# Residual sums by accumulating transfers in a hybrid decoder layer on one core

## The chip, the core and the metric

The kernel runs on one core of a Trainium2 chip. The metric is the device time of one execution in microseconds (us), the median of several runs. One execution was profiled; its views are quoted below. PE is TensorE (PEld its weight loads), DVE is VectorE, ACT is ScalarE, POOL is GpSimd, SP is SyncE, which here issues transfers only.

## The reference, cut to what matters

One decoder layer, 1024 tokens, width 1024, all in float32:

```python
a = rmsnorm(h, ln_pre_mix)                      # h = x
q, k, v, u, z = split(a @ w_in)
groups = concat([rmsnorm(dilated_attention(q, k, v)), rmsnorm(spatial_gating(u, z, ...))])
mixed = groups @ w_out
h = h + rmsnorm(mixed, ln_post_mix)             # residual sum 1
f = rmsnorm(h, ln_pre_ffn)
g, up = split(f @ w_gate_up)
y = (silu(g) * up) @ w_down
h = h + rmsnorm(y, ln_post_ffn)                 # residual sum 2
gate = sigmoid(h @ w_pe_gate + b_pe_gate)
out = h + gate * (p @ w_pe_proj)                # residual sum 3
```

The three lines with a residual sum are what the change touches.

## The kernel before

Tokens are handled in eight tiles of 128 rows (`t` = 0 to 7), each a [128, 1024] float32 tile of 512 KB. Every float32 matrix product is made of three fast passes: an operand is split into a rounded high part and a remainder (`split`, L430: a cast on ScalarE, a subtraction on VectorE), and `mm3` (L518) multiplies high by high, high by low and low by high. The large products (input, gate-up and down projections) also use a Strassen-like scheme with seven products on half blocks (`winograd_b`). PE therefore works through some 5600 matmuls, and the other engines prepare its operands and empty its banks.

The stages follow each other: input projection; spatial gating; attention in four head pairs, each first over the first 512 tokens (`first_half`) and then over the rest (`second_half`); gate-up; down projection; and the last stage with `ffn_out` and `embed`. Into the attention other work is fed as filler: the gating half of the output projection (`gated`), the embedding projection (`ple`), and, once tokens 0 to 3 are through `h_chain`, the early gate-up products (`first_products`).

Where the residual sums are made:

- `h_chain(t)` (L1018), after `attn_out(t)` has put the mixed rows of a tile into `part[t]`. It loads x from HBM, normalises the rows (`sumsq` on ScalarE, `rstd_from` with a power on POOL, `norm_apply` on VectorE), adds x on VectorE or POOL (`EITHER`), stores h to the HBM scratch `h1d`, and normalises again for the feed-forward part. Tiles 0 to 3 come in hooks in `second_half` of head pair 0 (`TODO`), tiles 4 to 7 after the attention. `F.first` and `F.second` then transpose the result on PE.
- `ffn_out(t)` (L1261) loads h back from `h1d`, normalises the down projection's rows `y`, adds h on VectorE, transposes y on PE (8 transposes) and splits it for the gate product.
- `embed(t, nh, ...)` (L1273) makes the gate product of a tile for one half of the columns (24 matmuls of 512 columns), adds the bias, takes the sigmoid, multiplies by the embedding rows, adds h2 (`y` after its sum) on VectorE, and stores the result.

The last stage runs `ffn_out` for tiles 0 to 3, `embed` for these tiles, `ffn_out` for tiles 4 to 7, `embed` for these; the final half of tile 7 is cut in two pieces of 256 columns.

The order of instructions on each engine isn't that of the code. The program first records all operations with their dependences (`Graph.call`). `price` (L176) gives each a cost on each engine that may run it, and `order` (L224) plays the program through with these costs: on every engine it takes the first recorded operation that is ready and whose buffers are to be had. What comes out is a fixed, in-order queue for each engine. An instruction that waits on the chip longer than the planner thought holds everything behind it on its engine. A transfer on SP is priced at 0.45 us of SP, then its bytes at 330 GB/s, one after another with all other transfers, and 3.0 us until it has landed; at most 8 are kept under way.

The lines in play: `price` L176, `order` L224, `load` L416, `tt` L421, `rstd_from` L496, `sumsq` L503, `norm_apply` L508, `h_chain` L1018, `rows_out` L1180, `ffn_out` L1261, `embed` L1273. All instructions are issued from one helper line, L383 (`issue`), so that the views tell them apart by engine, tile letter and shape: m is a [128, 1024] tile, s a [128, 512] one, p a PSUM bank, t a small statistic, d an HBM scratch tensor.

Of the kernel before, what the change touches and what calls it, by code (L numbers as in the profile page):

```python
# [17 lines left out]
P = 128  # L18
S = 1024
D = 1024  # L20
NT = S // P
# [12 lines left out]
ADD, SUB, MUL = ALU.add, ALU.subtract, ALU.mult  # L34
# [79 lines left out]
class Graph:  # L114
# [61 lines left out]
    def price(self, o, outs, ins):  # L176


        o.cost, o.port, o.table, o.bytes, o.sure = {}, {}, None, 0, 0.0
        n = max([v.n for v in outs[:1] + ins[:1]])  # L180
        for e in o.engines:
            port = False
            if e == "tensor":
                n = ins[1].n
                if o.what == "transpose":
                    busy, done = 0.110, 0.27
                elif ins[0].dt == F32R:
                    busy = max(0.110, (n + 32) / 2400.0)
                    done = n / 2400.0 + 0.18
                else:  # L190
                    busy = 0.222 if n <= P else n * 4 / 2400.0
                    done = busy + 0.16
            elif e == "vector":
                tensors = [v for v in ins if v.n > 4 or n <= 4]
                busy = n / 960.0 + 0.15
                if len(ins) > len(tensors) and n > 4:
                    busy += 0.06
                if o.what == "tensor_tensor_reduce":
                    busy += 0.083
                done = busy  # L200
                busy -= 0.06
                port = n > 16 and not any(v.psum for v in tensors) and bool(tensors)
            elif e == "scalar":
                done = n / 1200.0 + (0.16 if ins[0].psum else 0.19)
                busy = done - 0.08
                if isinstance(o.kw.get("bias"), Ref):
                    done, busy = done + 0.093, busy + 0.093
                if "accum_out" in o.kw:
                    done, busy = done + 0.1, busy + 0.09
                o.table = TABLES.get(next((a for a in o.args if isinstance(a, AF)), None))  # L210
            elif e == "gpsimd":
                if n > 16:
                    busy = 2.21e-3 * n + 0.15
                else:
                    busy = 0.2 if o.what == "tensor_scalar" else 0.4 + 0.15 * n
                done, port = busy, n > 16
            else:
                size = [v for v in outs + ins if isinstance(v, Ref) and v.buf.kind in "MSTC"][0]
                o.bytes = size.n * 4 * (size.parts[1] - size.parts[0])
                busy, done = 0.45, 0.0  # L220
            o.cost[e], o.port[e] = (busy, done), port


    def order(self):  # L224
# [19 lines left out]
        port, dma, table, lanes = 0.0, 1.5, 0, [0.0] * 8  # L244
        waiting = {e: [] for e in engines}
        coming, events = [], [0.0]
        done, first, picked = [False] * n, 0, []
# [55 lines left out]
        while left:  # L303
            if not events:
                raise ValueError(f"stuck at {ops[first].what} {first}")
            now = heapq.heappop(events)
            while events and events[0] <= now + 1e-9:
                heapq.heappop(events)
            while coming and coming[0][0] <= now + 1e-9:
                _, rank, i, e = heapq.heappop(coming)  # L310
                if ops[i].start is not None:
                    continue
                bisect.insort(waiting[e], (rank, i))
            for e in engines:
                if at[e] > now + 1e-9 or not waiting[e]:
                    continue
                o = pick(e, now)
                if o is None:
                    continue
                busy, took = o.cost[e]  # L320
                o.start, o.engine = now, e
                picked.append(o)
                if o.table and o.table != table:
                    busy, took, table = busy + 1.4, took + 1.4, o.table
                at[e] = now + busy
                if e == "sync":
                    dma = max(dma, now + 0.4) + o.bytes / 330e3
                    o.end = dma + 3.0
                    lanes = lanes[1:] + [o.end]
                    at[e] = max(at[e], lanes[0])  # L330
                else:
                    o.end = now + took
                if o.port[e]:
                    port = o.end
                    heapq.heappush(events, port)
                for x in o.engines:
                    if (o.rank, o.i) in waiting[x]:
                        waiting[x].remove((o.rank, o.i))
                o.new = [b for b in o.bufs if b.slot is None]
                for b in o.new:  # L340
                    b.slot = heapq.heappop(free[b.kind])[1]
                    group[b.group] = group.get(b.group, 0) + 1
                    b.ahead = first
                    early[b.kind][first : b.born] += 1
                for b in o.bufs:
                    b.left -= 1
                    b.until = max(b.until, o.end)
                    if not b.left:
                        heapq.heappush(free[b.kind], (b.until, b.slot))
                        group[b.group] -= 1  # L350
                        live[b.kind][b.born : b.last + 1] -= 1
                        early[b.kind][b.ahead : b.born] -= 1
                        heapq.heappush(events, b.until)
                done[o.i] = True
                left -= 1
                while first < n and done[first]:
                    first += 1
                for u in o.users:
                    u.waits -= 1
                    if not u.waits:  # L360
                        release(u)
                heapq.heappush(events, at[e])
                heapq.heappush(events, now + 0.02)
# [25 lines left out]
def hybrid_block(ctx: ExitStack, tc, a, out):  # L389
    G = Graph()  # L390

    def M(dt=F32, shape=(P, 1024), group=None):
        return G.buf("M", shape, dt, group)
# [22 lines left out]
    def load(dst, src, rate=1.0):  # L416
        o = G.call("sync", "dma_start", dst, src)
        o.bytes /= rate
        return o

    def tt(dst, x, y, op=ADD, engines="vector"):  # L421
        return G.call(engines, "tensor_tensor", out=dst, in0=x, in1=y, op=op)
# [11 lines left out]
    EITHER = ("vector", "gpsimd")  # L434
# [165 lines left out]
    x = a["x"][0]  # L600
# [39 lines left out]
    ppd, h1d = DR([S, D]), DR([S, D])  # L640
# [97 lines left out]
    for q, banks in in_products(2048, 1536, zu_mm):  # L738
        for i in range(4):
            if q in (1, 6, 5):  # L740
                v, t = {1: (zs, i), 6: (us, i), 5: (us, i + 4)}[q]
# [5 lines left out]
            else:  # L747
                v = {2: zs, 3: us}.get(q, us)[i + 4 * (q == 7)]
# [4 lines left out]
            if q in (3, 4):  # L753
                t = i + 4 * (q == 4)
# [24 lines left out]
    for q, banks in in_products(0, AW, qk_mm, (1, 2, 6, 5, 3, 7, 4)):  # L779
        for i in range(4):  # L780
            dst = {1: q_part[i], 2: q_part[i], 6: k_part[i][:, 0], 3: k_part[i][:, 0], 5: k_part[i][:, 1],
                   7: k_part[i][:, 1], 4: None}[q]
# [186 lines left out]
    ws, wa, part = [], [], {}  # L969
# [46 lines left out]
            dve("scalar_tensor_tensor", out=part[t][:, cs], in0=ps, scalar=rstd, in1=part[t][:, cs], op0=MUL, op1=ADD)  # L1016

    def h_chain(t):  # L1018
        xt, f, m = M(), M(), part[t]
        load(xt, x[t * P : (t + 1) * P, :])  # L1020
        norm_apply(m, m, rstd_from(sumsq(m, f), 1, D), gain["post"])
        tt(m, m, xt, ADD, EITHER)
        load(h1d[t * P : (t + 1) * P], m)
        norm_apply(f, m, rstd_from(sumsq(m, f), 1, D), gain["ffn"])
        kept[t] = f
# [233 lines left out]
    wpg = [[w for kk in range(2) for w in weights(piece_a(w_pg, nh * 512, kk))] for nh in range(2)]  # L1259

    def ffn_out(t):  # L1261
        y, h1, pp = acc[t], M(), M()
        load(h1, h1d[t * P : (t + 1) * P])
        load(pp, ppd[t * P : (t + 1) * P])
        norm_apply(y, y, rstd_from(sumsq(y, M()), 1, D), g_pf)
        tt(y, y, h1)
        hT = M(F32R, (P, 8, P)), M(F32R, (P, 8, P))
        for kk in range(2):
            hi, lo = (v[:, 4 * kk : 4 * kk + 4] for v in hT)
            split(hi, lo, transposed(y[:, kk * 512 : (kk + 1) * 512], 4))  # L1270
        return y, hT, pp

    def embed(t, nh, n, h2, hT, pp):  # L1273
        for c in range(0, 512, n):
            cs = slice(nh * 512 + c, nh * 512 + c + n)
            ps, gate = PB()[:, :n], SM()[:, :n]
            gemm(ps, [((hT[0][:, k], hT[1][:, k]), tuple(w[:, c : c + n] for w in wpg[nh][k])) for k in range(KT)])
            tt(gate, ps, b_pe[:, cs])
            act(gate, gate, AF.Sigmoid, after=[AFTER["silu"]])
            tt(gate, pp[:, cs], gate, MUL)  # L1280
            tt(gate, gate, h2[:, cs])
            load(out[0][t * P : (t + 1) * P, cs], gate)

    h2s = [ffn_out(t) for t in range(4)]
# [55 lines left out]
```

## Time and profile before

| what | value |
|---|---|
| median of 3 runs | 1178.31 us (1178.01 to 1178.48) |
| the profiled execution | 1178.0 us |
| its span, first to last instruction | 1176.2 us |
| granted TensorE clock, mean | 0.999 |
| DMA over the span | 208.77 MB, 177 GB/s |

In the views a row of instructions gives line, engine, operation, output tile `<-` input tiles, partitions by elements, `x` the count, then the busy time in us and the mean of one in ns, then the idle time of the engine just before and what ended it. A timeline row begins with start and length in us and merges neighbouring instructions of one kind (their parts may interleave with other rows). A row of windows gives the stretch, its length, and for PE, PEld, DVE, ACT and POOL the busy time and count, then the granted clock, the share of DMA busy time and GB/s. A DMA row gives KB of one transfer and the median us from issue to landing.

### The profile page before, as it was taken

How to read it: one execution, taken by the hardware profiler on the slowest of the kernel's cores; microseconds unless marked ns; L12 is line 12 of the kernel's file. 1: busy time of each engine (PE TensorE's matmuls, PEld its weight loads, DVE VectorE, ACT ScalarE, POOL GpSimd, SP SyncE). 2: the span in 40 equal slices, each digit the busy share in tenths (PEclk: the TensorE clock that was granted, in tenths of full speed). 3: DMA queues.
4: the chain of work that ended last, by engine and by line, in shares of the span. 5: the costliest groups of instructions: out<-in, count | busy, mean ns of one | idle time of the engine just before them, and what ended most of it. 6: DMA issues, size and time to landing. Idle time of an engine off the chain costs nothing.

```text
span 1176.2 us, 16341 instructions
## 1 busy us (share of the span) xinstructions
PE 1163.5 (99%) x5633; PEld 972.4 (83%) x5633; DVE 869.0 (74%) x1703; ACT 576.3 (49%) x1300; POOL 57.0 (5%) x68
## 2 busy tenths in 40 slices
PE   8999999999999999999999999999999999999998
PEld 6887888788878888888888888888888888888887
DVE  7888796566666676799888888887668965479653
ACT  8663436578768666566223222222344445357121
POOL 2101000000121000310000000000000000002000
PEclk9999999999999999999999999999999999999999
DMA  8224136999763996388455656544397223643111
GB/s 295 81 72 122 58 134 192 323 296 310 250 215 88 286 264 179 109 267 256 146 194 186 196 189 186 171 133 162 112 382 254 95 92 113 240 162 143 47 43 54
DMA packets 161244, 208.77 MB, mean 177 GB/s; under 512 B 12477, under 2 KB 89609, under 8 KB 161162
## 3 DMA queue, kind: packets, MB, share of 16 engines
q1 hardware_dynamic: 161162, 207.74, 55.4%
q8 instruction: 44, 0.72, 0.3%
q14 instruction: 38, 0.31, 0.1%
HBM read 147.63 MB, written 60.06 MB: 177 GB/s over the span
## 4 chain that ended last, share of the span: by engine, by line
PE 95%; DVE 2%; ACT 1%; DMA 1%; issue 0%; SPq 0%; POOL 0%; DVEq 0%; ACTq 0%
PE p L383 95%; DVE s L383 1%; ACT m L383 1%; DMA m<-in_w_in 1%; DVE t L383 1%; DMA d<-m 0%; DVE m L383 0%; SPq L383 0%; POOL m L383 0%; ACT s L383 0%; ACT t L383 0%; DVEq L383 0%; ACTq L383 0%
## 5 line engine op out<-in xcount | busy, mean ns | idle before, releaser
L383 PE MATMUL p<-m,m 128*128 128x512 f32 (+2 forms) x4620 | 1065.6, 388 | 1.9 <-DVE m L383 1.3
L383 PEld LDWEIGHTS p<-m,m 128*128 128x128 f32 x4620 | 848.0, 188 | 169.8 <-ACT m L383 2.0
L383 DVE TENSOR_TENSOR m<-m,m 128x512 fp32r<-128x512 f32 (+2 forms) x465 | 313.2, 707 | 70.5 <-ACT m L383 65.0
L383 ACT CAST m<-m 128x512 fp32r<-128x512 f32 x363 | 212.7, 622 | 192.8 <-PE p L383 148.1
L383 DVE TENSOR_TENSOR s<-p,s 128x512 f32<-128x512 f32 (+4 forms) x222 | 143.0, 655 | 85.9 <-PE p L383 58.4
L383 ACT ACTIVATE s<-s 128x512 f32<-128x512 f32 (+1 forms) x71 | 44.3, 626 | 218.0 <-DVE s L383 162.3
L383 DVE TENSOR_TENSOR m<-p,m 128x256 fp32r<-128x256 f32 (+3 forms) x132 | 61.5, 493 | 41.2 <-PE p L383 21.5
L383 POOL TENSOR_TENSOR t<-t,c 128x1 f32<-128x1 f32 (+1 forms) x56 | 42.0, 755 | 1012.4 <-ACT t L383 1002.9
L383 ACT COPY s<-p 128x512 f32<-128x512 f32 (+1 forms) x122 | 62.2, 517 | 44.0 <-PE p L383 43.0
L383 ACT CAST m<-s 128x256 fp32r<-128x256 f32 (+1 forms) x121 | 53.6, 480 | 29.3 <-PE p L383 15.6
L383 DVE TENSOR_TENSOR s<-s,s 128x512 f32<-128x512 f32 x88 | 60.7, 692 | 4.6 <-ACT s L383 0.7
L383 DVE TENSOR_TENSOR m<-s,m 128x256 fp32r<-128x256 f32 (+1 forms) x121 | 58.4, 511 | 6.9 <-ACT m L383 6.5
L383 PE MATMUL p<-c,m 128*128 128x128 f32 x328 | 49.7, 273 | 0.0
L383 ACT COPY m<-p 128x512 f32<-128x512 f32 (+1 forms) x72 | 31.5, 452 | 32.1 <-PE p L383 30.9
L383 PE MATMUL p<-c,s 128*128 128x128 f32 (+2 forms) x249 | 42.6, 282 | 2.4 <-DVE s L383 2.0
L383 PEld LDWEIGHTS p<-c,m 128*128 128x128 f32 x328 | 39.5, 140 | 5.9
L383 PE MATMUL p<-s,m 128*128 128x128 f32 (+1 forms) x256 | 43.8, 276 | 0.0
L383 ACT ACTIVATE m<-m 128x1024 f32<-128x1024 f32 x32 | 34.1, 1068 | 19.5 <-DVE m L383 15.0
L383 PEld LDWEIGHTS p<-c,s 128*128 128x128 f32 (+2 forms) x249 | 32.0, 145 | 11.4 <-DVE s L383 4.0
L383 PEld LDWEIGHTS p<-s,m 128*128 128x128 f32 x256 | 38.1, 190 | 3.2
L383 ACT ACTIVATE m<-m,t 128x384 f32<-128x384 f32 (+2 forms) x64 | 36.7, 578 | 4.9 <-DVE t L383 4.3
L383 ACT CAST m<-p 128x256 fp32r<-128x256 f32 (+1 forms) x80 | 34.4, 498 | 6.7 <-PE p L383 5.7
(58 smaller groups left out, 513.9 us busy)
## 6 DMA issues: line engine op xcount, KB each, us to landing
d<-s SPq DMA_DIRECT2D x149, 256.0 KB, 2.8
m<-d SPq DMA_DIRECT2D x51, 512.0 KB, 4.2
m<-in_w_gate_up SPq DMA_DIRECT2D x88, 256.0 KB, 3.9
m<-d SPq DMA_DIRECT2D x87, 256.0 KB, 7.2
s<-d SPq DMA_DIRECT2D x56, 256.0 KB, 4.2
d<-m SPq DMA_DIRECT2D x28, 512.0 KB, 5.4
m<-in_w_down SPq DMA_DIRECT2D x44, 256.0 KB, 6.1
m<-in_w_in SPq DMA_DIRECT2D x20, 512.0 KB, 3.9
```

The costliest lines, as they stand in the source:

```text
L383: getattr(getattr(nc, o.engine), o.what)(*[real(v) for v in o.args], **{k: real(v) for k, v in o.kw.items()})
```

## The change

Three groups of VectorE (or POOL) additions are replaced by transfers that add what they carry to what stands in the destination (`accum_op=ADD`); they are issued on POOL's queue. In `h_chain` x is no longer loaded into a tile of its own but added from HBM into the mixed rows. In `ffn_out` h is added from `h1d` into y. In `embed` h2 is added, from SBUF to SBUF, into the gated embedding for tiles 0 to 5; tiles 6 and 7 keep the addition on VectorE. `price` gets a cost for a transfer on POOL (1.0 us of POOL), `order` a landing time for it (bytes at 330 GB/s behind the other transfers, and 3.0 us). POOL's own arithmetic is priced as before.

```diff
@@ price
+            if o.what == "dma_start":
+                size = [v for v in outs + ins if isinstance(v, Ref) and v.buf.kind in "MSTC"][0]
+                o.bytes = size.n * 4 * (size.parts[1] - size.parts[0])
+                busy, done = (0.45 if e == "sync" else 1.0), 0.0
-            if e == "tensor":
+            elif e == "tensor":
@@ order
-                if e == "sync":
+                if o.what == "dma_start" and e == "gpsimd":
+                    dma = max(dma, now + 1.0) + o.bytes / 330e3
+                    o.end = dma + 3.0
+                elif e == "sync":
@@ hybrid_block
+    def add_from(dst, src):
+
+        return G.call("gpsimd", "dma_start", dst, src, accum_op=ADD)
@@ h_chain
-        xt, f, m = M(), M(), part[t]
-        load(xt, x[t * P : (t + 1) * P, :])
+        f, m = M(), part[t]
         norm_apply(m, m, rstd_from(sumsq(m, f), 1, D), gain["post"])
-        tt(m, m, xt, ADD, EITHER)
+        add_from(m, x[t * P : (t + 1) * P, :])
         load(h1d[t * P : (t + 1) * P], m)
@@ ffn_out
-        y, h1, pp = acc[t], M(), M()
-        load(h1, h1d[t * P : (t + 1) * P])
+        y, pp = acc[t], M()
         load(pp, ppd[t * P : (t + 1) * P])
         norm_apply(y, y, rstd_from(sumsq(y, M()), 1, D), g_pf)
-        tt(y, y, h1)
+        add_from(y, h1d[t * P : (t + 1) * P])
@@ embed
             tt(gate, pp[:, cs], gate, MUL)
-            tt(gate, gate, h2[:, cs])
+            if t < NT - 2:
+                add_from(gate, h2[:, cs])
+            else:
+                tt(gate, gate, h2[:, cs])
             load(out[0][t * P : (t + 1) * P, cs], gate)
```

More of the change, by code (lines that the diff above doesn't have):

```diff
@@ L210, in price @@
                 o.table = TABLES.get(next((a for a in o.args if isinstance(a, AF)), None))
-            elif e == "gpsimd":
+            else:
                 if n > 16:
@@ L216, in price @@
                 done, port = busy, n > 16
[L217 to L220, printed above, removed]
             o.cost[e], o.port[e] = (busy, done), port
@@ L1280, in embed @@
             tt(gate, pp[:, cs], gate, MUL)
-            tt(gate, gate, h2[:, cs])
+            if t < NT - 2:
+                add_from(gate, h2[:, cs])
+            else:
+                tt(gate, gate, h2[:, cs])
             load(out[0][t * P : (t + 1) * P, cs], gate)
```

## The prediction, made before the result was known

> **What bounds the kernel now.** I read the page first (engines, then the chain that ended last):
>
> ```profile
> PE 1163.5 (99%) x5633; PEld 972.4 (83%) x5633; DVE 869.0 (74%) x1703; ACT 576.3 (49%) x1300; POOL 57.0 (5%) x68
> PE 95%; DVE 2%; ACT 1%; DMA 1%; issue 0%; SPq 0%; POOL 0%; DVEq 0%; ACTq 0%
> ```
>
> PE is busy for 1163.5 of the 1176.2 us of the span; only 12.7 us are left in which it does nothing. VectorE, the engine that the change relieves most, is 26% idle. Where those 12.7 us lie, the windows by stage say (length, then busy time of PE, PEld, DVE, ACT, POOL):
>
> ```profile
> 0.00:20.00 20.00, 15.28 (x50) 10.16 (x51) 12.66 (x23) 14.43 (x33) 4.66 (x9) 1.00 0.88 323
> 20.00:300.00 280.00, 278.28 (x1431) 234.85 (x1429) 218.09 (x545) 166.94 (x403) 18.45 (x19) 1.00 0.58 183
> 300.00:400.00 100.00, 98.19 (x555) 83.12 (x554) 62.54 (x154) 71.41 (x201) 13.46 (x18) 1.00 0.64 190
> 400.00:1171.00 771.00, 771.00 (x3601) 643.79 (x3600) 574.41 (x980) 323.11 (x668) 20.45 (x22) 1.00 0.53 171
> 1171.00:1177.00 6.00, 0.73 (x7) 0.53 (x5) 1.27 (x3) 0.42 (x1) 0.00 (x0) 0.76 0.13 45
> ```
>
> The start has 4.7 us without PE work, 20 to 300 has 1.7, 300 to 400 has 1.8, the end 4.5; from 400 to 1171 us PE has no gap at all, at a granted clock of 1.00. So VectorE's time is not what ends the run. The change can gain only in a stage where it acts and PE idles, which is 300 to 400 us: 1.8 us at most. What it can lose is open: each sum becomes a transfer, and a transfer has a latency that PE may have to wait for. The forecast is therefore a matter of finding the places where PE has nothing else to do while a sum is in flight.
>
> **The change part by part.** The engine work that goes:
>
> ```profile
> L383 DVE TENSOR_TENSOR m<-m,m 128x1024 f32<-128x1024 f32 x12 | 14.7, 1224 | 0.3
> L383 POOL TENSOR_TENSOR m<-m,m 128x1024 f32<-128x1024 f32 x4 | 9.6, 2407 | 7.2 <-issue 4.8 <-PE p L383 2.5
> L383 DVE TENSOR_TENSOR s<-s,m 128x512 f32<-128x512 f32 x15 | 10.4, 691 | 0.5
> ```
>
> The 16 wide sums are the 8 of `h_chain` (4 of them on POOL) and the 8 of `ffn_out`; of the 15 narrow ones of `embed` 12 go (tiles 0 to 5, two halves). That is 14.7 + 12 x 0.691 = 23.0 us of VectorE and 9.6 us of POOL. Neither is on PE's path after 400 us, so this is worth nothing by itself there. Bytes from HBM stay the same: the 16 loads of x and h1 move from SP's queue to POOL's and read the same 512 KB each; 12 transfers of 256 KB inside SBUF are new.
>
> The price of one accumulating transfer is not in this trace; the nearest rows (KB each, median us from issue to landing; the first and third of the page, the second of 1060 to 1085 us with its bandwidth line):
>
> ```profile
> m<-d SPq DMA_DIRECT2D x51, 512.0 KB, 4.2
> m<-in_x SPq DMA_DIRECT2D x16, 512.0 KB, 9.7
> ```
>
> ```profile
> GB/s 0 0 0 0 0 0 0 0 13 0 0 52 216 419 387 387 347 315 361 334 374 420 413 374 406 420 419 406 426 203 46 13 0 0 0 0 0 0 0 0
> m<-d SPq DMA_DIRECT2D x8, 512.0 KB, 7.5
> ```
>
> A plain 512 KB load took 4.2 us, and 7.5 us with eight in flight at about 400 GB/s. An add that costs nothing more than a load is the lower bound, 4.2 us. The upper one is 7.5 plus 2.4 for an issue on POOL as dear as POOL's own wide add: 9.9 us. I take 6.3 us as an estimate: 4.2, plus 1.25 for reading the target as well (512 KB at 420 GB/s), plus 0.8 for the issue, near POOL's small operations below. Successive adds then cannot land closer than 2.5 us (two reads each).
>
> [...]
>
> The place that matters is the boundary between the down projection and the last stage. PE, then POOL, then VectorE:
>
> ```profile
> 1059.74 17.62 PE L383 MATMUL p<-m,m 128*128 128x512 f32 x77
> 1077.20 3.65 PE L383 MATMUL p<-c,m 128*128 128x128 f32 x32
> 1080.61 43.78 PE L383 MATMUL p<-m,m 128*128 128x512 f32 x192
> ```
>
> ```profile
> 1068.24 1.06 POOL L383 TENSOR_TENSOR t<-t,c 128x1 f32<-128x1 f32 x2 [559.11 <-ACT t L383]
> 1070.62 2.35 POOL L383 TENSOR_TENSOR t<-t,c 128x1 f32<-128x1 f32 x2 [1.31 <-ACT t L383]
> ```
>
> ```profile
> 1068.83 1.28 DVE L383 SCALAR_TENSOR_TENSOR m<-m,t,m 128x1024 f32<-128x1024 f32 x1 [1.27 <-POOL t L383]
> 1070.15 1.23 DVE L383 TENSOR_TENSOR m<-m,m 128x1024 f32<-128x1024 f32 x1
> ...
> 1076.20 1.28 DVE L383 SCALAR_TENSOR_TENSOR m<-m,t,m 128x1024 f32<-128x1024 f32 x1
> ...
> 1077.52 1.23 DVE L383 TENSOR_TENSOR m<-m,m 128x1024 f32<-128x1024 f32 x1
> 1079.09 4.88 DVE L383 TENSOR_TENSOR m<-p,m 128x512 fp32r<-128x512 f32 x8 [0.35 <-ACT m L383]
> ```
>
> Down-projection matmuls end at 1077.2, the 32 transposes of tiles 0 to 3 follow, the gate matmuls start at 1080.6, with no gap. Tile 0 is summed at 1071.4, tile 3 at 1078.75, just in time. After the change the normalisations follow one another without the sums: tile 0 still ends at 1070.1, tile 1 at 1071.4, tiles 2 and 3 some 1.7 and 3.0 us later, since their power (POOL, 0.5 to 1.2 us each) now shares POOL's in-order queue with the issues of adds 0 and 1. Landing at 6.3 us and 2.5 us apart: 1076.4, 1078.9, 1081.4, 1083.9. PE transposes tile 0 at 1077.2 (8 of 32, 0.9 us), then waits for tile 1 until 1078.9, and is done with it at 1079.8. Tile 0's splits are ready by then (half of its transposes 0.45, a cast of about 0.6, a subtraction of 4.88 / 8 = 0.6: 1078.9), so its gate matmuls (192 / 8 = 24, 43.78 / 8 = 5.5 us) cover tiles 2 and 3. Loss: 1079.8 - 1077.2 - 1.8 = 0.8 us, if the written order has tile 0's matmuls ahead of tile 2's transposes. If all four tiles' transposes go first, it is 1083.9 + 0.9 - 1077.2 - 3.65 = 4.0 us; with adds 1.3 us apart instead, some 0.3. The planner prices an add at 1.0 us of POOL, 1.6 of transfer and 3.0 behind, one after another, which is near my spacing, so it should put matmuls between. I take +1.5 us, with ends 0 and 4.
>
> [...]
>
> Tiles 4 to 7 of `ffn_out` are added from 1084 on and transposed at 1124: 27 us of cover or more, cost 0. The 12 gate sums are followed only by their stores:
>
> ```profile
> 1151.82 0.69 DVE L383 TENSOR_TENSOR s<-s,m 128x512 f32<-128x512 f32 x1
> 1171.77 0.42 DVE L383 TENSOR_TENSOR s<-p,m 128x256 f32<-128x256 f32 x1 [1.08 <-PE p L383]
> ```
>
> The last one (tile 5) starts at 1151.8, 20 us before PE's end; behind the store that waits for it on SP there are only later stores. Cost 0, and the end is unchanged, as tiles 6 and 7 keep VectorE.
>
> `h_chain` of tiles 4 to 7 lies at 485 to 510 us:
>
> ```profile
> 476.23 29.08 PE L383 MATMUL p<-m,m 128*128 128x512 f32 x127
> 505.15 1.03 PE L383 MATMUL p<-c,m 128*128 128x128 f32 x8
> 505.94 11.14 PE L383 MATMUL p<-m,m 128*128 128x512 f32 x48
> 516.92 1.03 PE L383 MATMUL p<-c,m 128*128 128x128 f32 x8
> ```
>
> PE has the early gate-up products as filler, and takes one tile's transposes only every 11.8 us. Each add is 5 us later than a sum (6.3 - 1.2); a delay of that size disappears in the 48 matmuls between two tiles. Cost 0; without that cover it would be 5 us once.
>
> `h_chain` of tiles 0 to 3 lies inside the attention at 309 to 360 us. PE's waits there, from 200 to 400 us (in total, times, longest):
>
> ```profile
> PE p L383 <- DVE m L383: 1.8, 3, 0.7
> PE p L383 <- DVE s L383: 0.8, 1, 0.8
> PE p L383 <- ACT m L383: 0.3, 1, 0.3
> ```
>
> VectorE is what PE waits for, and sums go from it: a gain of up to 1.8 us. Against that, each tile adds two waits: SP's store of h1 waits for the add with the attention's loads queued behind it, and ScalarE's second sum of squares waits for it with PSUM copies and casts for PE behind it. Both are put where the planner expects the landing (5.6 us or more after the normalisation); if it is late by 4.3 us (9.9 - 5.6), each of four tiles can hold ScalarE that long. No row prices that; ends -1.8 and +6, and I take -0.3, near the waits that are there.
>
> Sum: +1.5 - 0.3 = +1.2 us. The profiled execution took 1178.0 us (span 1176.2), 0.3 below the median of 1178.31: 1178.3 + 1.2 = **1179.5 us**.
>
> **The rivals.** *A wait at the boundary (slower).* It decides once an add takes over 7.1 us from the end of tile 0's normalisation (1077.2 - 1070.1). At 9.9 us tile 0 lands at 1080.0, its matmuls can start 1.7 us later (the transposes, cast and subtraction above), 1081.7 - 1077.2 - 0.9 = 3.6 us lost, and up to 2.5 for each later tile that the written order has ahead of them: +4 to +9, 1182 to 1187. For it: 7.5 us with transfers in flight, and the four loads of the projected embeddings still run there. Against: h1's four loads are gone from just before. If POOL rather than the DMA engines did the adding, so that the change doesn't do what it says, POOL's 2.4 us row makes it this case too. Chance 0.23.
>
> *A wait in the attention (slower).* ScalarE or SP behind late adds at 309 to 360 us, where the in-order queues feed PE most directly: about 1 us of PE for each tile after what is hidden, +4, 1182. For it: loads of x took 9.7 us. Against: in that window no wait of PE is put down to a DMA. It decides when adds there take over 6 to 7 us. Chance 0.14.
>
> *The stalls of 300 to 400 us go and the boundary is hidden (lower end).* 1178.3 - 1.8 = 1176.5, still within 0.2%; more needs a start or end that shrinks, which no row offers. Chance 0.08.
>
> **How the numbers follow.** About 0.2%, 2.4 us, is what a measurement of this kernel can tell from no change. The forecast (0 to 2.4 us around +1.2; own range 1178.0 to 1180.6) has 0.55 and lies within it. The two slower rivals give 0.37. The last gives 0.05 for faster by over 0.2% (for schedules I can't foresee) and 0.03 within: 0.05, 0.58, 0.37. The range goes from 1176.5 to 1185.0: all but the far half of the boundary rival and the strays below.
>
> **What would show it.** Right: PE without a gap from 400 us to the boundary, a gap of 1 to 2 us between the down projection's last matmul and the gate's first, VectorE 23 us less busy, the tail as it was, adds of 512 KB landing in about 6 us and 2.5 apart. Wrong: gaps of several us at the boundary with PE or its loads waiting for an accumulate; ScalarE or SP waiting on accumulates at 300 to 360 us with PE idle behind; POOL busy for over 2 us per transfer; or a time below 1176, which would mean that VectorE bound PE in a way these views don't show.

## The result, and the profile after

The changed kernel takes **1187.0 us** (median of 6 runs, 1186.1 to 1189.7); the kernel before takes 1178.4 us in the same session. The ratio is 1.0074, with a 95% interval of 1.0063 to 1.0084: slower by 7.4 to 9.9 us. The forecast of 1179.5 us was 7.5 us too low, and its range ended at 1185.0. The profiled execution took 1187.6 us against 1178.0 before.

The page of the changed kernel, first the busy time of the engines, then POOL's own DMA queue (packets, MB, share of 16 engines' span), then the chain that ended last:

```profile
PE 1167.2 (98%) x5633; PEld 974.6 (82%) x5633; DVE 845.6 (71%) x1679; ACT 573.3 (48%) x1300; POOL 69.3 (6%) x92
q0 software_dynamic: 4032, 11.54, 5.5%
PE 91%; DMA 4%; DVE 2%; ACT 2%; issue 1%; POOL 0%; SPq 0%; ACTq 0%; POOLq 0%
```

VectorE is relieved by 23.4 us (23.0 were worked out). PE has the same 5633 instructions, but the chain that ends last now runs for 4% of the span through transfers, where it had 1%.

Where the time went, the windows by stage tell. To be set beside the five rows of before:

```profile
0.00:20.00 20.00, 15.31 (x46) 10.66 (x47) 13.04 (x25) 15.06 (x35) 4.64 (x9) 1.00 0.89 329
20.00:300.00 280.00, 278.28 (x1430) 235.06 (x1429) 216.33 (x538) 165.21 (x398) 17.55 (x19) 1.00 0.58 181
300.00:400.00 100.00, 96.73 (x539) 81.53 (x538) 59.55 (x149) 68.31 (x196) 13.29 (x20) 1.00 0.68 180
400.00:1060.00 660.00, 658.10 (x3054) 547.57 (x3054) 501.71 (x892) 288.20 (x604) 10.89 (x16) 1.00 0.60 186
1060.00:1100.00 40.00, 37.50 (x175) 31.16 (x174) 26.19 (x34) 22.92 (x50) 12.09 (x16) 0.96 0.58 131
```

Up to 300 us nothing has changed. From 300 to 400 us PE idles 3.3 us in place of 1.8. From 400 to 1060 us, where it had no gap, 1.9 us are missing. Around the boundary to the last stage 2.5 us are missing, and the granted clock (the third number from the right) is 0.96 on average.

The span of the profiled execution grew by 9.6 us (1185.8 - 1176.2), and PE's own milestones divide it: 5.0 had arisen when the transposes of the last stage began (1082.2 in place of 1077.2), 3.2 came between these and the gate matmuls, 1.4 behind that. Idle time explains 3.3 of the first 5.0; for the rest PE was busy 1.7 us longer over as many matmuls (5161) at a clock of 1.00, and no view says why.

**The boundary**, PE of the changed kernel. These rows answer to the three of before, in which the transposes began at 1077.20 and the gate matmuls 3.41 us later:

```profile
1082.20 1.91 PE L386 MATMUL p<-c,m 128*128 128x128 f32 x16
1085.18 1.06 PE L386 MATMUL p<-c,m 128*128 128x128 f32 x8 [1.07 <-ACT m L386]
1087.68 1.47 PE L386 MATMUL p<-c,m 128*128 128x128 f32 x8 [1.43 <-DMA m<-d]
1088.80 3.39 PE L386 MATMUL p<-m,m 128*128 128x512 f32 x8
```

The gate matmuls begin 6.60 us after the first transpose, 3.2 later than in the rhythm of before. I call this difference the gap below. All 32 transposes stand ahead of the gate matmuls in PE's order, so the last of the four tiles holds everything. The wait ahead of the third tile ends with an add too: the view puts it down to ScalarE, but the third add was issued at 1074.9 and landed 10.1 us later, at 1085.0, just before these transposes. The add of the fourth, from the chain of waits between 1070 and 1095 us:

```profile
1080.40 7.14 DMA m<-d
1087.55 0.14 issue
1087.68 7.47 PE p L386 x29
```

Its normalisation had ended long before (start and length, VectorE, then POOL's issues of the four adds):

```profile
1070.63 4.87 DVE L386 SCALAR_TENSOR_TENSOR m<-m,t,m 128x1024 f32<-128x1024 f32 x4
```

```profile
1072.54 1.84 POOL L386 DMA_DIRECT2D m<-d  x2 [1.42 <-DVE m L386]
1074.92 0.86 POOL L386 DMA_DIRECT2D m<-d  x1 [0.54 <-issue]
1080.40 0.88 POOL L386 DMA_DIRECT2D m<-d  x1 [4.62 <-PE p L386]
```

From the end of the normalisation (1075.5) to the landing (1087.5) the fourth sum takes 12.0 us, where VectorE took 1.2. The transfers are the reason, as the GB/s row of 1060 to 1092 us (40 slices of 0.8 us) with the queue's share of this window shows:

```profile
GB/s 10 0 0 0 0 0 0 10 0 0 0 0 148 266 348 415 394 425 358 215 169 164 215 200 220 220 200 215 200 220 200 220 205 46 0 0 0 0 0 0
q0 software_dynamic: 576, 2.10, 34.5%
```

The loads run at 348 to 425 GB/s, the adds at 200 to 220. Four adds take 34.5% of 32 us, 2.76 us each, one after another without a pause until about 1086.5.

And what follows on the gap: PE's busy time and granted clock (the columns after the length) in steps of 2 us:

```profile
1084.00:1086.00 2.00, 0.93 (x10) 1.00 1.04 207
1086.00:1088.00 2.00, 0.57 (x6) 1.00 0.32 61
1088.00:1090.00 2.00, 2.00 (x10) 0.55 0.00 0
1090.00:1092.00 2.00, 2.00 (x7) 0.60 0.00 0
1092.00:1094.00 2.00, 2.00 (x10) 1.00 0.00 0
```

After 4 us in which PE was 38% busy it works for 4 us at little over half the clock: 2 x 0.45 + 2 x 0.40 = 1.7 us more, some 0.3 of it still within the gap.

**The attention.** ScalarE's waits of the changed kernel from 300 to 440 us (total, times, longest), those of the two transfers:

```profile
ACT m L386 <- DMA m<-in_x: 4.8, 3, 2.3
ACT m L386 <- DMA m<-in_w_gate_up: 3.2, 2, 2.4
```

The first row is the adds of x; the second is raw weights of the early gate-up products, behind which PE idles at 400 to 435 us, where no add is in flight. So two causes are possible here: the adds, or a new order of the work around them. The experiments part them.

### The profile page after: what moved, and what is told of

Read it like the earlier page. It is cut to its first block, busy times and chain, and to the rows that moved or that the text cites. A ratio compares the mean times of both kernels' runs of the same rounds, so it can differ in the third digit from the quotient of the medians.

```text
span 1185.8 us, 16367 instructions
## 1 busy us (share of the span) xinstructions
PE 1167.2 (98%) x5633; PEld 974.6 (82%) x5633; DVE 845.6 (71%) x1679; ACT 573.3 (48%) x1300; POOL 69.3 (6%) x92
## 4 chain that ended last, share of the span: by engine, by line
PE 91%; DMA 4%; DVE 2%; ACT 2%; issue 1%; POOL 0%; SPq 0%; ACTq 0%; POOLq 0%
PE p L386 91%; ACT m L386 2%; DMA m<-in_x 1%; DVE s L386 1%; DMA m<-in_w_gate_up 1%; ACT s L386 1%; DMA m<-d 1%; DVE m L386 1%; DMA d<-t 1%; DVE t L386 1%; POOL t L386 0%; SPq L386 0%; ACT t L386 0%; ACTq L386 0%; POOLq L386 0%
## 5 line engine op out<-in xcount | busy, mean ns | idle before, releaser
L386 PE MATMUL p<-m,m 128*128 128x512 f32 (+3 forms) x4620 | 1069.7, 389 | 1.7 <-DVE m L386 1.3
L386 DVE TENSOR_TENSOR m<-m,m 128x512 fp32r<-128x512 f32 (+1 forms) x453 | 296.9, 688 | 67.9 <-ACT m L386 62.8
L386 DVE TENSOR_TENSOR s<-p,m 128x512 f32<-128x512 f32 (+1 forms) x17 | 11.2, 660 | 46.1 <-PE p L386 46.0
L386 DVE SCALAR_TENSOR_TENSOR m<-m,t,m 128x1024 f32<-128x1024 f32 x24 | 30.4, 1280 | 13.9 <-POOL t L386 13.8
```

The source lines that it names most:

```text
L386: getattr(getattr(nc, o.engine), o.what)(*[real(v) for v in o.args], **{k: real(v) for k, v in o.kw.items()})
```

## The experiments

Two places (attention and boundary), and at each several causes that the trace alone can't part. Where it is said that a kernel has every instruction in its order, each engine's list is the same but for the rows named. The kernel before took 1178.3 to 1178.6 us beside them. Fourth landing and gap are those of the boundary; the landing is counted from the first transpose (in the changed kernel 1087.5 - 1082.2 = 5.3), the gap as before from the first transpose to the gate matmuls, less 3.41 us.

| run | us | ratio, 95% interval | 4th landing | gap |
|---|---|---|---|---|
| the change | 1187.0 | 1.0063 to 1.0084 | +5.3 | 3.2 |
| e1 row sums only | 1182.4 | 1.0022 to 1.0044 | | |
| e2 y sums only | 1183.5 | 1.0026 to 1.0051 | +5.4 | 3.8 |
| e3 gate sums only | 1178.1 | 0.9987 to 1.0005 | | |
| e4 3072 bytes | 1185.7 | 1.0045 to 1.0073 | +5.8 | 3.4 |
| e5 rows, stand-in on VectorE | 1180.1 | 1.0003 to 1.0024 | | |
| e6 rows, old order | 1208.9 | 1.0245 to 1.0272 | | |
| e7 y, plain loads | 1178.5 | 0.9995 to 1.0012 | +0.6 | 0.0 |
| e8 y, other loads moved | 1179.5 | 1.0000 to 1.0017 | +2.7 | 0.2 |
| e9 the late parts only | 1178.1 | 0.9989 to 1.0007 | | |
| e10 rows, dearer price | 1188.6 | 1.0064 to 1.0094 | | |
| e11 rows, plain loads | 1178.9 | 0.9994 to 1.0012 | | |
| e12 all, other loads moved | 1185.9 | 1.0049 to 1.0075 | +4.9 | 2.4 |
| e13 y, other loads left out | 1181.2 | 1.0016 to 1.0037 | +4.2 | 1.8 |
| e14 all, plain loads | 1179.7 | 1.0005 to 1.0023 | +0.5 | 0.0 |
| e15 all, other loads left out | 1185.6 | 1.0046 to 1.0072 | +3.7 | 1.2 |

### Which of the three sums

e1 keeps the transfer in `h_chain` alone, e2 in `ffn_out`, e3 in `embed`; the other two are as before.

> Only the eight sums of x with the mixed rows are left to accumulating transfers; h goes to y and h2 to the gated embedding on VectorE as before. Theory A (two places): of the 8.6 us about 4 to 5 arise between 310 and 440 us, where ScalarE and SP stand behind these adds and the first-product weights come late, and the rest at the last stage's boundary: this run 1182 to 1183.5, and its last stage begins without a gap of TensorE. Rival C (the boundary alone; the gaps at 310 to 440 us are made up by slack later): 1178 to 1179.5. Rival B (any new order of the planner costs what the change costs, whatever is moved): also above 1182, but then the run with the gate sums alone as well.

> Only the eight sums of h with y are left to accumulating transfers. Theory A: the boundary costs 3 to 4.6 us (the wait for the fourth tile's add, then matmuls at a lower granted clock): 1181.5 to 1183, with the matmuls of 310 to 440 us where the kernel before has them. Rival C: 1186 to 1187.5, the whole loss. Rival D (at the boundary only the wait counts and the lower clock is a chance of one run): 1180.5 to 1181.5.

> Only the twelve sums of h2 with the gated embedding are left to accumulating transfers. Theory A: nothing waits for them but the store of the output, which no later work needs: 1178 to 1179. Rival B (any new order costs): above 1182. Rival E (POOL's issues take VectorE's and each other's time in the last stage): 1179.5 to 1181.

e1 costs 2.6 to 5.2 us, e2 3.1 to 6.0, e3 nothing. The medians are 3.9 and 5.0 above before, 8.9 together, and the whole change is 8.6. So theory A holds: two places that add up. Rival B falls with e3, rival C with e1, and E with e3. The last stage of e1 begins without a gap (transposes at 1082.87, gate matmuls 3.41 later). The last expected point of e2 is answered by its trace, which shows the gap and the slow stretch a second time. So rival D falls too, and the time lies even 0.5 us above theory A's range:

```profile
1077.16 1.91 PE L386 MATMUL p<-c,m 128*128 128x128 f32 x16
1080.26 1.06 PE L386 MATMUL p<-c,m 128*128 128x128 f32 x8 [1.19 <-DMA m<-d]
1082.74 1.94 PE L386 MATMUL p<-c,m 128*128 128x128 f32 x8 [1.42 <-DMA m<-d]
1084.33 6.04 PE L386 MATMUL p<-m,m 128*128 128x512 f32 x22
```

```profile
1080.00:1082.00 2.00, 1.06 (x8) 1.00 0.76 150
1082.00:1084.00 2.00, 1.26 (x6) 0.63 0.00 0
1084.00:1086.00 2.00, 2.00 (x8) 0.51 0.00 0
```

### What holds the fourth add at the boundary

POOL was free at 1075.8 and issued the fourth add only at 1080.4, just after the first had landed at 1080.1 (7.6 us after its issue). The kernel is built with `dynamic_dma_scratch_size=1024`, taken here for the room of the descriptors of POOL's transfers (no view shows a descriptor), so three adds in flight might be all that fit. e4 raises it to 3072, with every instruction in its order:

```diff
-    nc = bacc.Bacc("TRN2", target_bir_lowering=False, num_devices=1, dynamic_dma_scratch_size=1024)
+    nc = bacc.Bacc("TRN2", target_bir_lowering=False, num_devices=1, dynamic_dma_scratch_size=3072)
```

> The changed kernel, every engine's instructions in the same order, with 3072 bytes instead of 1024 for the descriptors of POOL's transfers. Theory R (the fourth add of the boundary was issued 4.6 us after POOL was free because only three adds' descriptors fit): it is issued at about 1076, lands at about 1083, no gap is left ahead of the gate matmuls and the clock stays at 1.00: 1182.5 to 1184. Theory Q (it is the transfers: four adds of 2.76 us each, with the queue at 1.0 of the 16 engines' time from 1071 to 1086 us, so that an earlier issue only waits elsewhere): the fourth still lands at about 1087: 1186 to 1187.5.

POOL's issues in e4, and the share of its queue from 1060 to 1092 us:

```profile
1073.73 1.84 POOL L386 DMA_DIRECT2D m<-d  x2 [1.31 <-DVE m L386]
1076.11 0.86 POOL L386 DMA_DIRECT2D m<-d  x1 [0.54 <-DVE m L386]
1077.41 0.88 POOL L386 DMA_DIRECT2D m<-d  x1 [0.43 <-issue]
```

```profile
q0 software_dynamic: 576, 2.10, 33.9%
```

The size did hold the issue: the fourth now follows after 0.43 us of idle time, in place of 4.62. But the add then takes 11.9 us and lands no earlier (+5.8 against +5.3): it only waits elsewhere, as theory Q had it. The time, just below theory Q's range, is 1.3 us below that of the change, and the intervals overlap. The gap is as long as before, yet the clock stayed at 1.00. In the profiled execution that does not show in the time (1187.7): behind the gap it takes 1.4 us less than the change, but its transposes begin 1.3 us later.

e7 takes the accumulation away and nothing else: e2 with every instruction in its order.

```diff
-        add_from(y, h1d[t * P : (t + 1) * P])
+        G.call("gpsimd", "dma_start", y, h1d[t * P : (t + 1) * P])
```

> The kernel with the sums of h and y alone by transfer (1183.5), every engine's instructions in its order; each transfer is a plain load of h over y, so that the normalised y is left out of the sum. Theory H (the gap at the boundary is four transfers that take 2.76 us of the queue each, twice what a plain load takes): the fourth lands some 5 us earlier, the gap goes: 1177.5 to 1179.5. Theory L (it is the way over POOL's queue: issue, start and landing, however fast the bytes move): 1181.5 to 1183.5.

PE of e7, and both queues from 1060 to 1085 us, in which four 512 KB loads of each kind fall:

```profile
1077.58 3.65 PE L386 MATMUL p<-c,m 128*128 128x128 f32 x32
1080.99 11.37 PE L386 MATMUL p<-m,m 128*128 128x512 f32 x49
```

```profile
q1 hardware_dynamic: 576, 2.10, 23.3%
q0 software_dynamic: 576, 2.10, 23.0%
```

No gap and no loss, as theory H has it: the same transfers, on the same queue, from the same engine, take 0.23 x 25 / 4 = 1.44 us each without the accumulation, against 2.76 with it, and the same as SP's. Theory L falls. POOL's way costs nothing here; the halved rate is what costs.

### What else shares the queue there

In e2 four plain loads (the embedding's projected rows, 512 KB each, SP's queue) run just ahead of the adds. e8 and e12 were to put them behind, by splitting `ffn_out` into two loops and letting the planner start the loads after the last add (in short):

```diff
-        load(pp, ppd[t * P : (t + 1) * P])
...
+            G.call("sync", "dma_start", pp, ppd[t * P : (t + 1) * P], after=[last])
```

> The kernel with the sums of h and y alone by transfer; the loads of the embedding's rows (512 KB a tile) are taken from ahead of the adds and put behind the last add of each four tiles; TensorE's order is unchanged. Theory H, with the queue as the place: four plain loads of 1.3 to 1.6 us stand between the norms and the adds' landing, so the fourth lands 3 to 5 us earlier, and the gap shrinks to under 1 us: 1179 to 1181. Theory L: 1182.5 to 1184.

> The whole change, with the loads of the embedding's rows put behind the last add of each four tiles, all else in its order. If the two places add up: 1187.0 less what that move gave with the y sums alone (1183.5 to 1179.5), 1182.5 to 1183.5, with no gap at the boundary and the clock at 1.00. If the later start of the adds here (1072.5 against 1067.5 us) leaves too little time even so: 1184.5 to 1186.

Neither did what it was to do. The planner's `after` moves a load in SP's order, but nothing makes it wait there, and SP had nothing else to issue. In e8 all four loads are still ahead of the adds (issues of SP, then of POOL, with the matmuls):

```profile
1064.15 3.04 SPq L386 DMA_DIRECT2D m<-d  x4
```

```profile
1069.06 1.98 POOL L386 DMA_DIRECT2D m<-d  x2 [3.77 <-issue]
1071.38 0.87 POOL L386 DMA_DIRECT2D m<-d  x1 [0.34 <-issue]
1074.89 0.90 POOL L386 DMA_DIRECT2D m<-d  x1 [2.64 <-issue]
```

```profile
1080.28 3.89 PE L386 MATMUL p<-c,m 128*128 128x128 f32 x32
1083.93 6.40 PE L386 MATMUL p<-m,m 128*128 128x512 f32 x27
```

What did change is that loads and adds come earlier against PE: the first add is issued 11.2 us before the first transpose, not 9.7 as in e2, and the loads 16.1 before it, not 13.4. The fourth add lands at +2.7 in place of +5.4, the gap is 0.2 us, and 3.9 us come back (1183.5 to 1179.5). So e8 tells how near the edge the boundary is: adds that start 1.5 us earlier, behind loads that start 2.7 us earlier, are the difference between a covered wait and an open one. In e12 the first add is 11.2 us ahead as well, but two of the loads were issued at 1077 to 1080 us and shared the queue with the adds; the fourth landed at +4.9, and the time fell by 1.1 us only, within the two intervals.

e13 and e15 leave the loads out instead (e2 and the whole change, every other instruction in its order); VectorE then multiplies by a tile that is there already (in short):

```diff
-            tt(gate, pp[:, cs], gate, MUL)
+            tt(gate, b_pe[:, cs], gate, MUL)
```

> The kernel with the sums of h and y alone by transfer (1183.5), every engine's instructions in its order, without the eight loads of the embedding's rows (VectorE multiplies a tile that is there already, so the embedding is left out of the output). If those plain loads, issued 4 us ahead of the adds, hold them up in the queue: the four adds have it to themselves, the fourth lands about 3 us earlier (1079.5 in place of 1082.6), the gap of TensorE is under 0.5 us: 1179 to 1180.5. If the adds hold up only one another: the fourth lands within 1 us of where it did, 1182.5 to 1184.

> The changed kernel, every engine's instructions in its order, without the eight loads of the embedding's rows (left out of the output). If they share the queue with the adds, as in the run with the sums of h and y alone: three adds land about 3 us earlier and with them the release of the fourth: the gap shrinks and 3 to 4.5 us come back: 1182.5 to 1184. If they do not matter: 1186 to 1187.5.

The fourth lands 1.2 and 1.6 us earlier, less than the 3 expected; the gap halves or better (1.8 and 1.2), and the times are 2.3 and 1.4 us lower, each with intervals that still overlap. Both times lie between the two ranges expected. The adds hold up mainly one another. The fourth add of e13 was issued at 1073.5, again right behind the landing of the first (1066.8 + 6.5 = 1073.3).

### The rows of the attention

e5 has every instruction of e1 in its order, and VectorE adds a tile that lies ready where the transfer stood; e11 has plain loads there; e6 keeps the order of before and puts the transfer where the engine's sum stood; e10 tells the planner a dearer price. The edits in short:

```diff
e5   o = add_from(m, x[...]), issued as
+    nc.vector.tensor_tensor(out=m, in0=m, in1=gain["post"], op=ADD)
e11
-    add_from(m, x[t * P : (t + 1) * P, :])
+    G.call("gpsimd", "dma_start", m, x[t * P : (t + 1) * P, :])
e6   load(xt, ...) not issued, and tt(m, m, xt, ADD, EITHER) issued as
+    nc.gpsimd.dma_start(m, x[t * P : (t + 1) * P, :], accum_op=ADD)
e10
-    add_from(m, x[t * P : (t + 1) * P, :])
+    add_from(m, x[t * P : (t + 1) * P, :]).bytes *= 2
```

> The kernel with the row sums alone by transfer (1182.4), every engine's instructions in its order; in the place of each of the eight transfers VectorE adds a tile that is there already, so that x is left out of the output and nothing waits for a transfer. Theory W (the 3.9 us are waits for the adds to land and what follows from them): 1178 to 1179.5, and the matmuls of 310 to 440 us without the gaps. Theory P (they come from the order that the planner gives when it counts on the transfers): 1181.5 to 1183.

> The kernel before, every engine's instructions in its order, but the loads of x left out and each of the eight sums done by an accumulating transfer in the place where the engine's sum stood. Theory W: 1182 to 1186, since that order leaves some 1.2 us for a sum that takes 5.7 to 7. Theory P: 1178 to 1180.

> The kernel with the row sums alone by transfer (1182.4), every engine's instructions in its order; each transfer is a plain load of x over the rows, so that the normalised rows are left out of the sum. If the waits at 310 to 375 us come from the halved rate (1.3 to 1.5 us of the landing): about 1180 to 1181, since ScalarE waited 0.3 to 2.4 us for three of these adds. If they come from the way over POOL's queue whatever the rate: 1182 to 1183. The 1.6 us that the planner's order costs stay in both.

> The kernel with the row sums alone by transfer (1182.4), but the planner counts each add's bytes twice, so that it allots 7.2 us in place of 5.6 from issue to landing; 5.7 to 7.0 were measured. If the 1.9 us of waits at 310 to 375 us come from a plan that allots too little: they shrink, 1180 to 1181.5. If no plan can hide the landings of tiles 0 to 3 at that place, or if the new order costs elsewhere: 1182 or more.

Without the wait (e5) 1180.1, without the accumulation (e11) 1178.9; the interval of e11 lies below that of e1, that of e5 just overlaps it (0.9994 to 1.0012 and 1.0003 to 1.0024 against 1.0022 to 1.0044). The time of e5 lies between the ranges of its two theories, and e11 came out below both of its own. In windows, first before, then e1, e5 and e11 (length, then PE's busy time):

```profile
310.00:375.00 65.00, 63.19 (x346) 53.04 (x345) 40.74 (x92) 45.88 (x132) 13.12 (x18) 1.00 0.49 149
375.00:440.00 65.00, 65.00 (x394) 56.34 (x393) 43.50 (x145) 44.63 (x132) 0.00 (x0) 1.00 0.98 267
```

```profile
310.00:375.00 65.00, 61.84 (x339) 51.74 (x337) 37.91 (x90) 43.89 (x129) 12.79 (x20) 1.00 0.64 167
375.00:440.00 65.00, 62.41 (x362) 52.81 (x362) 39.27 (x121) 40.46 (x116) 0.47 (x1) 1.00 0.91 239
```

```profile
310.00:375.00 65.00, 63.74 (x352) 53.83 (x351) 44.68 (x102) 45.71 (x135) 8.98 (x15) 1.00 0.43 134
375.00:440.00 65.00, 62.81 (x369) 53.17 (x368) 37.59 (x112) 40.84 (x114) 0.00 (x0) 1.00 0.97 257
```

```profile
310.00:375.00 65.00, 62.98 (x346) 53.05 (x345) 40.04 (x95) 44.80 (x132) 11.46 (x19) 1.00 0.55 166
375.00:440.00 65.00, 64.00 (x378) 54.34 (x377) 38.42 (x117) 41.86 (x117) 0.00 (x0) 1.00 0.95 258
```

From 310 to 375 us e1 loses 1.35 us, e5 gains 0.55: the adds' waits are worth 1.9 us there. From 375 to 440 us, where no add is in flight, e1 loses 2.6 and e5 2.2, at the same weights: that part comes with the planner's new order, not with a wait for an add there. e11, in the same order, loses 1.0. So the order has a price, but no steady one: 0.4 to 2.8 us by the time of e5, -0.7 to 1.4 by that of e11. How the rest moves from run to run I can't settle; one way is the clock, which in the profiled executions of e8 and e9 was 0.97 from 310 to 375 us, some 2 us, and both took 2 us more than the medians of their kernels.

e6 shows what a plan that knows nothing of the landing pays: 30 us, far more than either theory expected. ScalarE, PE's waits for it (300 to 600 us):

```profile
ACT m L389 <- DMA m<-in_x: 38.4, 8, 8.6
```

```profile
PE p L389 <- ACT s L389: 16.0, 5, 5.9
```

Not all of the 30 us is idle time: from 300 to 600 us PE is idle for 22.9 us, and the granted clock, down to 0.52 from 330 to 340 us, is worth some 8 more.

The planner's price for the transfer thus saves most of the loss. But a price nearer the truth (7.2 us) does not save the rest: e10 is at 1188.6, 6 us worse than e1. Its waits for the adds do shrink (ScalarE 2.6 us at 310 to 375, against 5.6), but PE loses 2.3 us behind late weights at 375 to 440 us, and 2.2 us after that:

```profile
375.00:440.00 65.00, 62.67 (x342) 53.13 (x341) 34.88 (x109) 38.25 (x107) 0.00 (x0) 0.93 0.86 231
```

PE's idle time from 310 to 600 us is only 1 us above that of e1 (6.8 against 5.8). The larger part is the clock in this row (the third number from the right): 0.93 in place of 1.00 over 62.67 us of work is some 4 us. "The new order costs elsewhere" is what came true.

### What is left when the accumulation goes, and what is free

e14 is the changed kernel, every instruction in its order, with `accum_op=ADD` struck out of `add_from`; e9 leaves only the late parts to transfers: tiles 4 to 7 of `h_chain` and `ffn_out`, and the gate sums.

> The changed kernel, every engine's instructions in its order, all 28 accumulating transfers as plain loads of the same bytes, so that each residual replaces what it was to be added to. If the halved rate is the whole loss and the two places add up: 1187.0 less 3.5 at the rows and 5.0 at the boundary, 1178.5 to 1179.5. If the order that the planner gives costs by itself: 1180 to 1181. If the parts do not add up, since the boundary of the whole change starts its adds later: above 1181.

> The sums that the forecast priced at nothing, and only these, by transfer: x to the mixed rows and h to y for tiles 4 to 7, h2 to the gated embedding; tiles 0 to 3 of the first two on an engine as before. If their covers hold: 1177.5 to 1179. If the transfers of any of them are waited for, or if any other order of the planner costs: 1180 or more. Faster than the kernel before by over 2.4 us only if VectorE's freed 14 us are worth something by themselves, which nothing so far shows.

e14 lies between the first two of its ranges: it is 0.6 to 2.7 us above before, in place of 7.4 to 9.9: the accumulation is 7.4 of the 8.6 us, by the medians. e9 costs nothing, and gains nothing either, though VectorE is 16.6 us less busy (852.4 in place of 869.0). It is the best version that keeps transfers, level with the kernel before (1178.1 against 1178.3), and no run points to a version that beats both.

## Why the prediction was wrong, point by point

- **What bounds the kernel** was right: PE, and VectorE's freed time is worth nothing by itself (e3 and e9: 7.4 and 16.6 us of VectorE less, and no change). Of the stall of the attention that could go, at most 0.55 us went (310 to 375 us in e5 and e14, nothing in e11), not 1.8.
- **The rate of the adds** was nearly right: 2.5 us apart by the estimate, 2.76 measured, 1.44 without the accumulation. The rate is 0.52 of the plain load's (1.44 / 2.76, e7); that the transfer reads its target as well, for which the estimate added 1.25 us, no run shows. The price of one add, 6.3 us from the normalisation's end, was a little low for adds that do not follow at once on one another (issue to landing 6.0 to 6.5 in the median for the adds of x in the change, e1 and e9, and 0.65 from the normalisation to the issue), and far too low where four follow on loads: 8.2 us for the first, 12.0 for the fourth.
- **The boundary is one step that failed.** "The planner ... should put matmuls between. I take +1.5 us, with ends 0 and 4." It did not put any between: all 32 transposes stand first, which the same paragraph prices at 4.0 us. The gap was 3.2, and 3.8 in e2. The new order could not be seen in the trace of before, but the one row at hand, the 32 transposes of before ahead of its gate matmuls, spoke for the dearer case, and the estimate went to the better one. Its reason, that the planner's spacing (1.6 us of transfer) is near its own 2.5, does not hold either: 2.76 were measured. That the planner left no matmuls between because it counted on landings in time is likely, but no run shows it. The lower clock behind the gap, 1.7 us, was in no step. The rival "a wait at the boundary" (chance 0.23, +4 to +9) is what happened: e2 costs 5.0. But it decided at another tile. The text's point was the first add, over 7.1 us from its normalisation; with the new order that normalisation ended 10.3 us ahead of the transposes, and the add, at 8.2, was in time. The fourth ended 6.7 us ahead (1082.2 - 1075.5) and took 12.0.
- **`h_chain` of tiles 0 to 3 is the other.** "No row prices that; ends -1.8 and +6, and I take -0.3." It is +3.9 (e1). The two waits that the text named are there: ScalarE waits 4.8 us for adds, and SP's stores hold its queue for 6.2 us from 354. The rival "a wait in the attention" (chance 0.14, 1182) has the size right. (The 9.7 us that it has for x's loads is the median of the whole run, its start included; the two loads issued between 295 and 365 us took 6.8.) That a planner with a price for the landing gives another order, in which weights come late at 400 to 435 us, when the last add has long landed, was in no step.
- **The two slower rivals were taken to exclude each other.** 0.23 and 0.14 were chances of one or the other; both came, 1178.4 + 5.0 + 3.9 = 1187.3, and the range, which left out the far half of the first, held neither that nor 1187.0.
- **The covers held**: tiles 4 to 7 of both, and the gate sums, cost nothing (e9, e3). The issue on POOL takes 0.86 to 0.92 us, the first one 1.06, against 0.8 estimated.

## What to carry to other kernels

In this kernel an accumulating transfer was free where PE had other work for 17 us or more from its issue to the transposes of the sum (tile 4 of `h_chain` in the changed kernel: 492.6 to 510.2 us), or where only a store waited for it, and dear where the next stage begins with it. There the bytes in flight count at 0.52 of the plain rate, one transfer after another (2.76 us for each 512 KB add), up to the last that the reader's in-order queue needs. Look for the order of that queue before choosing between "hidden" and "not hidden"; if it can't be seen, the dearer case belongs in the middle of the forecast. Two rivals at different places of a kernel do not exclude each other, and the range has to hold their sum. And after waits of this kind look at the granted clock as well as at the idle time: in e6 it costs some 8 us, in e10 some 4.

## What the runs showed of the hardware that was not expected

- A 512 KB accumulating transfer takes 2.76 us of the DMA engines' time, and a plain one from the same engine 1.44 (e7); POOL is busy 0.88 us for the issue of the one and 0.54 for the other.
- With `dynamic_dma_scratch_size` at 1024 POOL held the fourth 512 KB add back until the first had landed (4.6 us of idle time, which the profile puts down to PE); at 3072 it did not (0.43 us, e4). It changed where the add waited, not when it landed.
- The granted clock fell behind gaps that were not empty. In the change and in e2 it went to between 0.51 and 0.63 (means of 2 us) for 3 to 4 us after 4 us of PE with 1.4 to 1.5 us of work in them, and no single wait over 1.5 us. In e4, with only 1.1 us of work in its emptiest 4 us (1085.45 to 1089.45) and waits as long (1.48 and 1.44 us), it stayed at 1.00: what decides is not settled here.
